# Query transposes moved into the score banks, two blocks at a time, and the second key head's stacks written in halves

## The chip, the cores and the metric

The kernel runs on one core of a Trainium2 chip. The metric is the device time of one execution in microseconds (us), lower is better; times below are medians of several executions. A core has a matrix engine (TensorE, PE in the rows, with its weight loads as PEld), a vector engine (VectorE, DVE), an activation engine (ScalarE, ACT), GpSimd (POOL) and a queue that issues transfers (SyncE, SP). PE writes its results into PSUM, eight banks of 512 float32 columns by 128 partitions; ACT and DVE read them from there. Each engine works through its own instructions in order.

## What is computed

Two layers of a decoder trunk over 1024 tokens with 16 meta tokens in front, 1040 rows of 1024 features, in float32. Cut to what matters:

```python
h = jnp.concatenate([jnp.broadcast_to(meta.astype(x.dtype)[None], (B, N_META, x.shape[-1])), x], axis=1)
for l in range(DEPTH):                      # DEPTH = 2
    h = hybrid_layer(h, cos, sin, ...)
return h[:, N_META:]

def hybrid_layer(x, ...):
    h = rms_norm(x, norm_g)
    z = h @ w_in                            # 1024 x 6408
    aq, ak, av, ag, mq, mk, mv, mi, mf, mo, mgate = jnp.split(z, split_points(), axis=-1)
    q = apply_partial_rope(rms_norm(aq, q_norm_g), cos, sin)    # 16 heads of 64
    k = apply_partial_rope(rms_norm(ak, k_norm_g), cos, sin)    # 2 key heads of 64
    ya = sliding_window_sink_attention(q, k, v, sink) * jax.nn.silu(ag)
    ...                                     # mLSTM on mq, mk, mv, gated: ym
    return x + jnp.concatenate([ya, ym], axis=-1) @ w_out

# sliding_window_sink_attention, for each block of 128 queries:
scores = einsum(qb, kb) * scale             # keys: 16 meta tokens, the block before, the block itself
scores = where(mask, scores, NEG)
m = maximum(scores.max(-1), sink_b)
e = exp(scores - m)
probs = e / (e.sum(-1) + exp(sink_b - m))
out = einsum(probs, vb)
```

## The kernel before

**Numbers as pairs.** Every float32 factor of a large product is split into a high part, rounded to the matrix engine's format fp32r, and a low part, the remainder. A product of two such pairs is three matmuls (high by high, high by low, low by high). ACT makes the high part by a copy, DVE or POOL the low part by a subtraction that reads the same source.

**Stages.** A layer runs: keys and values of all tokens (`kv_tasks`), then the attention of eight pairs of heads, then the mLSTM of four heads, then the output product. While the attention of one pair runs, PE also computes projections for later work: the gate of a pair of heads (`g_tasks`) beside even pairs, the queries of the next two pairs (`q_tasks`) beside odd ones, the mLSTM values beside pair 7. `weave` lays the two lists of tasks into each other, 24 or 25 foreground tasks (6 to 9 projection matmuls each) over one pair's steps, and PE's instructions stay in that order. The instructions of ACT, DVE and POOL are ordered by a scheduler when the program is built.

**One block of attention.** A pair has 9 blocks of 128 queries in layer 0 (block 0 is the 16 meta tokens), 8 in layer 1. For block b, `s1` writes the scores of both heads into one of two score tiles `S` (each two banks, one a head: four matmuls, L667), DVE puts the mask and the sink into them (L670, L681) and takes the maximum (L685), ACT makes the exponentials and their sum (L688), DVE the reciprocal (L690), ACT scales (L693). Two steps later `s2` transposes the probabilities into the one bank `T` (L704, L707), from which ACT (L711, L712) and DVE (L714, L715) make high and low parts. One step after that `s3` and `s4` multiply them with the values into the one bank `O` (L731, L743), from which ACT (L746) and DVE (L748) take the result. `s1` of block b + 2 writes the same score tile as block b. Of a score bank's 512 columns, 274 at most hold scores.

**PSUM.** Two banks are `S` tile 0, two `S` tile 1, one is `T`, one `O`, and two, named `pj`, take turns for everything else: the projections, and also the query transposes. A gate chunk is taken from its `pj` bank by a tanh on ACT and L640 on DVE.

**Queries.** `q_stacks(j, g)` makes the stationary operand of four blocks' scores for pair j: four transposes of 128 by 128 into one `pj` bank (L617), then `q_put`: two ACT copies of 64 partitions by 512 columns (L600, L601) and two DVE subtractions (L602, L603). It is called at foreground tasks 20 or 21 for the next pair's first half (g = 0, blocks 1 to 4) and 8 or 9 for the second (g = 1, blocks 5 to 8). The 16 meta queries go by a small transpose into columns of the `O` bank (L622) and the same four lines at 16 columns.

**Keys.** The key stacks `Ks` hold one of the two key heads at a time, both halves of the partitions. The second head's, for pairs 4 to 7, are written over the first's near the end of pair 3: `k_stacks(1, g, i)` is an ACT copy (L436) and a DVE subtraction (L437) of 64 partitions by 576 columns, four calls, after the scores of blocks (3, 6), (3, 7), (4, 1), (4, 2), with (pair, block) as in the source.

## Time and profile before

| what | us |
|---|---|
| median of 3 runs | 1950.03 (1949.86 to 1952.85) |
| the profiled execution | 1953.92 |
| its span, first to last instruction | 1952.2 |
| PE busy in it | 1908.1 (98%) |
| DVE, ACT, POOL busy | 1088.3, 1067.7, 906.4 |

The profiled execution is 3.89 us above the median of the three runs, and 1.72 us of it lie outside the span. Its granted TensorE clock is 0.998 over the span. In rows of the trace "idle before <- releaser" is the time for which an engine stood still before an instruction, and the engine and line that ended the wait. A PE row such as `x6` merges six matmuls of one form; a PE row's duration runs past the start of the next, since matmuls are pipelined.

### The profile page before, as it was taken

The page shows a single profiled execution, that of the slowest core. Times are in us where ns is not written, and L with a number is a line of the kernel's source. Part 1 is how long each engine was busy: PE and PEld are TensorE (multiplying, and loading weights), DVE is VectorE, ACT ScalarE, POOL GpSimd, SP SyncE. Part 2 cuts the span into 40 slices and gives each one's busy share as a digit, 9 for nine tenths or more (in the row PEclk, how much of TensorE's full clock was granted, in tenths as well). Part 3 has the DMA queues.
Part 4 walks back from the last instruction along what each step waited for, and adds up shares of the span by engine and source line. Part 5 has one row for each costly group of instructions (what it writes and reads, how often), then busy time and mean ns, then how long its engine had stood idle before and what let it go on. Part 6 is the DMA issues. An engine that isn't in the chain of part 4 may idle for free.

```text
span 1952.2 us, 36164 instructions
## 1 busy us (share of the span) xinstructions
PE 1908.1 (98%) x12827; PEld 1799.7 (92%) x12827; DVE 1088.3 (56%) x2966; ACT 1067.7 (55%) x3133; POOL 906.4 (46%) x1102
## 2 busy tenths in 40 slices
PE   8999999999999999999999999999999999999999
PEld 7998898999999999977789999999999999998887
DVE  7777777667454363532445678776673635437211
ACT  6577776747454544643334777776464535446221
POOL 3544544336545454564325345444365444547332
PEclk9999999999999999999999999999999999999999
DMA  4111111121222121455541111112122121226543
GB/s 153 44 37 49 39 43 35 37 65 35 62 60 58 41 56 55 146 164 168 176 132 50 39 37 54 43 36 59 39 58 64 40 67 50 57 62 187 171 149 121
DMA packets 150838, 148.28 MB, mean 76 GB/s; under 512 B 15081, under 2 KB 123921, under 8 KB 150658
## 3 DMA queue, kind: packets, MB, share of 16 engines
q1 hardware_dynamic: 150658, 145.97, 25.5%
q8 instruction: 101, 1.65, 0.4%
q14 instruction: 79, 0.65, 0.1%
HBM read 122.58 MB, written 23.29 MB: 75 GB/s over the span
## 4 chain that ended last, share of the span: by engine, by line
PE 80%; DVE 6%; ACT 4%; issue 3%; POOL 3%; DMA 3%; SPq 0%; POOLq 0%; DVEq 0%; ACTq 0%
PE pj L186 35%; PE pj L226 13%; PE pss L1204 6%; PE pj L1204 6%; PE po L1204 5%; PE po L917 2%; PE S L667 2%; PE pss L917 2%; DMA raw<-in_w_in_dram 2%; PE O L743 2%; POOL RING L160 1%; PE O L731 1%; PE pt L917 1%; ACT t L688 1%; PE T L707 1%
## 5 line engine op out<-in xcount | busy, mean ns | idle before, releaser
L186 PE MATMUL pj<-H,RING 128*128 128x384 f32 (+2 forms) x3456 | 583.0, 322 | 0.0
L186 PEld LDWEIGHTS pj<-H,RING 128*128 128x128 f32 x3456 | 543.3, 188 | 2.5 <-issue 0.2
L160 POOL TENSOR_TENSOR RING<-raw,RING 128x512 fp32r<-128x512 f32 (+1 forms) x192 | 255.5, 1338 | 121.5 <-ACT RING L159 114.4
L226 PE MATMUL pj<-RING,H 128*128 128x256 f32 (+1 forms) x1920 | 268.3, 286 | 3.5 <-DVE u L640 3.5
L226 PEld LDWEIGHTS pj<-RING,H 128*128 128x128 f32 x1920 | 242.5, 189 | 4.0 <-DVE u L640 3.8
L226 PE MATMUL pj<-H,RING 128*128 128x384 f32 (+2 forms) x1152 | 215.0, 326 | 3.9 <-DVE u L603 3.9
L186 PE MATMUL pj<-RING,H 128*128 128x256 f32 x1536 | 209.9, 287 | 3.3 <-DVE H L300 1.6
L178 POOL TENSOR_TENSOR RING<-raw,RING 128x512 fp32r<-128x512 f32 x96 | 125.9, 1318 | 175.8 <-ACT RING L177 167.3
L186 PEld LDWEIGHTS pj<-RING,H 128*128 128x128 f32 x1536 | 193.8, 191 | 6.1 <-DVE H L300 2.1
L226 PEld LDWEIGHTS pj<-H,RING 128*128 128x128 f32 x1152 | 179.4, 189 | 4.8 <-PE T L707 2.3
L177 ACT ACTIVATE RING<-raw 128x512 fp32r<-128x512 f32 x128 | 80.7, 631 | 173.0 <-DMA raw<-in_w_out_dram 139.6
L159 ACT ACTIVATE RING<-raw 128x512 fp32r<-128x512 f32 (+1 forms) x196 | 122.8, 630 | 66.1 <-DMA raw<-in_w_in_dram 50.4
L752 POOL TENSOR_TENSOR u<-u,w1k 128x128 f32<-128x128 f32 (+1 forms) x136 | 63.7, 468 | 172.7 <-DVE w1k L748 168.6
L688 ACT ACTIVATE t<-S,mx 128x145 f32<-128x145 f32 (+1 forms) x272 | 100.3, 373 | 59.8 <-DVE mx L685 52.7
L718 POOL TENSOR_SCALAR_AFFINE_SELECT p<-p 128x512 fp32r<-128x512 f32 x112 | 72.4, 646 | 126.9 <-DVE p L714 126.4
L930 POOL TENSOR_TENSOR p<-u,p 128x258 fp32r<-128x258 f32 x64 | 49.7, 777 | 170.8 <-ACT p L929 155.6
L1204 PE MATMUL pss<-RING,H 128*128 128x512 f32 x384 | 120.5, 394 | 0.0
L1204 PE MATMUL pj<-RING,H 128*128 128x512 f32 x352 | 110.7, 396 | 0.0
L693 ACT ACTIVATE t<-t,mx 128x144 f32<-128x144 f32 (+1 forms) x272 | 97.5, 407 | 20.3 <-DVE mx L690 20.1
L866 DVE SCALAR_TENSOR_TENSOR t<-u,cw,t 128x384 f32<-128x384 f32 (+1 forms) x144 | 107.2, 744 | 2.2
L886 DVE SCALAR_TENSOR_TENSOR t<-t,pj 128x384 f32<-128x384 f32 (+2 forms) x48 | 24.5, 511 | 124.8 <-ACT t L885 124.7
L748 DVE TENSOR_TENSOR w1k<-O,w1k 64x128 f32<-64x128 f32 (+1 forms) x272 | 74.6, 274 | 34.2 <-ACT w1k L746 31.3
(344 smaller groups left out, 3804.6 us busy)
## 6 DMA issues: line engine op xcount, KB each, us to landing
raw<-in_w_out_dram SPq DMA_DIRECT2D x128, 256.0 KB, 2.8
raw<-in_w_in_dram SPq DMA_DIRECT2D x100, 256.0 KB, 2.8
raw<-in_w_in_dram SPq DMA_DIRECT2D x192, 128.0 KB, 2.3
spool<-u SPq DMA_DIRECT2D x56, 192.0 KB, 1.9
p<-x SPq DMA_DIRECT2D x24, 256.0 KB, 3.6
t<-spool SPq DMA_DIRECT2D x30, 192.0 KB, 3.4
p<-spool SPq DMA_DIRECT2D x26, 192.0 KB, 4.2
u<-em SPq DMA_DIRECT2D x8, 576.0 KB, 6.5
```

The source lines that it names most:

```text
L159: sc.activation(hi, raw[:, :, 0:o], AF.Copy)
L160: eng.tensor_tensor(lo, raw[:, :, 0:o], hi, op=ALU.subtract)
L177: sc.activation(hi, raw, AF.Copy)
L178: (ve if i > 8 and i % 2 else gp).tensor_tensor(lo, raw, hi, op=ALU.subtract)
L186: last = pin(pe.matmul(out, a, b, start=(i == 0), stop=(i == n - 1)))
L226: pin(pe.matmul(out(), x, y, start=(k + i == 0), stop=(k == n - 1 and i == 2)))
L688: sc.activation(P[:p, 145 * h:145 * h + 145], S[:p, h, 1 + 127 * h:146 + 127 * h], AF.Exp, bias=mx[:p, 0, h:h + 1], accum_out=mx[:p, 1, h: ...
L693: sc.activation(Pn, Pn, AF.Copy, scale=mx[:p, 2, h:h + 1])
L748: ve.tensor_tensor(y[64 * h:64 * h + 64, :p], O[0:64, p * h:p * h + p], up[0:64, p * h:p * h + p], op=ALU.add)
L866: ve.scalar_tensor_tensor(z, RAW[:, t0 + i:t0 + i + n], wcol(i), z, ALU.mult, ALU.add)
L917: pin(f(*a, **k))
L1204: pin(pe.matmul(ps[:p, :], a, b, start=(i + n == 0), stop=(i == 15 and n == len(terms) - 1)))
```

## The change

Two things are moved. First, all of `q_stacks` but the very first of a layer becomes `q_turn` and `q_take`, called from `s1`: behind the score matmuls of a block named in `visits`, two transposes write the unused columns 384 to 512 of that block's two score banks, and once the block's softmax has been issued two ACT copies and two DVE subtractions of 64 partitions by 2 x 128 columns take them. A visit comes two blocks ahead of the first of the two blocks that it serves: blocks 8 of the pair before, 1, 3 and 5. There are 30 visits in each layer in place of 15 calls of `q_stacks`, with the same 60 transposes. Second, `k_stacks` takes a first block and a count, and the second key head is written in eight calls of 288 columns, after the scores of blocks (3, 6), (3, 7), (3, 8) and (4, 1) to (4, 5), by the table `KEYS`. As each is a task of the woven list, the foreground tasks of pairs 3 and 4 shift by one against the steps in places.

```diff
--- before.py
+++ after.py
@@ -34,6 +34,8 @@
 UW = 1152
 NPAIR = 8
 EARLY = 80
+KEYS = {(3, 6): (0, 2, 0), (3, 7): (0, 2, 1), (3, 8): (2, 2, 0), (4, 1): (2, 2, 1),
+        (4, 2): (4, 2, 0), (4, 3): (4, 2, 1), (4, 4): (6, 2, 0), (4, 5): (6, 2, 1)}
 FIRST = ((0, 0), (0, 1), (1, 0))
 
 
@@ -427,14 +429,14 @@
                 pin(pe.transpose(ps[:, 128 * i:128 * i + 128], KR[:, 4 * g + 1 + i, :], ident))
             sc.activation(KT[:, 4 * g:4 * g + 4, 16:144], ps[:, 0:512].rearrange("p (a c) -> p a c", a=4), AF.Copy)
 
-        def k_stacks(kv, g, i):
+        def k_stacks(kv, a, n, i):
 
             s0 = 64 * kv
-            src = KT[s0:s0 + 64, 4 * g:4 * g + 4].rearrange("p a c -> p (a c)")
+            src = KT[s0:s0 + 64, a:a + n].rearrange("p a c -> p (a c)")
             d = 64 - s0 if i else s0
-            hi, lo = [T[d:d + 64, 576 * g:576 * g + 576] for T in Ks]
+            hi, lo = [T[d:d + 64, 144 * a:144 * a + 144 * n] for T in Ks]
             sc.activation(hi, src, AF.Copy)
-            ve.tensor_tensor(lo, src, Ks[0][s0:s0 + 64, 576 * g:576 * g + 576], op=ALU.subtract)
+            ve.tensor_tensor(lo, src, Ks[0][s0:s0 + 64, 144 * a:144 * a + 144 * n], op=ALU.subtract)
 
         def v_stacks(kv, g):
 
@@ -617,6 +619,22 @@
                 pin(pe.transpose(ps[:, 128 * i:128 * i + 128], X[:, 256 * i + c0:256 * i + c0 + 128], ident))
             q_put(U[:, 0:1024], ps, 512)
 
+        def q_turn(S, j, g, i):
+
+            c0 = 128 * (j % 2)
+            X = A[j]["q"]["X", g == 1]
+            for k in range(2):
+                pin(pe.transpose(S[:, k, 384:512], X[:, 256 * (i + k) + c0:256 * (i + k) + c0 + 128], ident))
+
+        def q_take(S, j, g, i):
+
+            Q = q_unit(j, g)[:, 0:1024].rearrange("p (h a c) -> p h a c", h=2, a=4)[:, :, i:i + 2]
+            src = S[:, :, 384:512]
+            sc.activation(Q[0:64, 0], src[0:64], AF.Copy)
+            sc.activation(Q[64:128, 1], src[64:128], AF.Copy)
+            ve.tensor_tensor(Q[64:128, 0], src[0:64], Q[0:64, 0], op=ALU.subtract)
+            ve.tensor_tensor(Q[0:64, 1], src[64:128], Q[64:128, 1], op=ALU.subtract)
+
         def q_meta_turn(j, ps):
             c0 = 128 * (j % 2)
             pin(pe.transpose(ps, A[j]["q"]["XM"][:, c0:c0 + 128], ident[:16, :16]))
@@ -657,6 +675,7 @@
             def s1(b):
                 t0, p = TT[b]
                 S = SS[blk[0] % 2]
+                visit = visits.get(blk[0])
                 blk[0] += 1
                 k0, kn, o = (0, 16, 128) if b == 0 else (0, 144, 128) if b == 1 else (16 + (b - 2) * 144, 272, 0)
                 for h in range(2):
@@ -666,6 +685,8 @@
                     for i in range(2):
                         pin(pe.matmul(S[:p, h, o + 2 - 2 * h:o + 2 - 2 * h + kn], lq, Ks[i][:, k0:k0 + kn],
                                   start=(i == 0), stop=(i == 1)))
+                if visit:
+                    q_turn(S, *visit)
                 if st.setdefault("S", 0) < 2:
                     ve.tensor_copy(cols(S, 1, 783, 1), snk[:, l, 2 * j:2 * j + 2].rearrange("p (h c) -> p h c", c=1))
                 st["S"] += 1
@@ -691,6 +712,8 @@
                 for h in range(2):
                     Pn = P[:p, 1 + 144 * h:145 + 144 * h]
                     sc.activation(Pn, Pn, AF.Copy, scale=mx[:p, 2, h:h + 1])
+                if visit:
+                    q_take(S, *visit)
                 live[b] = P
 
             def s2(b):
@@ -1052,8 +1075,8 @@
         in_order[0] = True
         fq = q_tasks(0, wq[0], QQ[0])
         n0 = len(fq) - 24
-        at = {n0 + 6: [lambda: k_turn(0), lambda: (k_stacks(0, 0, 0), k_stacks(0, 0, 1)), lambda: v_stacks(0, 0)],
-              n0 + 15: [lambda: k_turn(1), lambda: (k_stacks(0, 1, 0), k_stacks(0, 1, 1)), lambda: v_stacks(0, 1)],
+        at = {n0 + 6: [lambda: k_turn(0), lambda: (k_stacks(0, 0, 4, 0), k_stacks(0, 0, 4, 1)), lambda: v_stacks(0, 0)],
+              n0 + 15: [lambda: k_turn(1), lambda: (k_stacks(0, 4, 4, 0), k_stacks(0, 4, 4, 1)), lambda: v_stacks(0, 1)],
               n0 + 21: [lambda: q_stacks(0, 0, "pss")] + ([lambda: q_meta(0, bank("po")[:, 0:16])] if first_q == 0 else [])}
         at[n0 + 12] = q_post(QQ[0], False)
         for i, f in enumerate(fq):
@@ -1065,6 +1088,8 @@
         SS[:] = [bp["S"].tile([128, 2, 512], F32, name=f"S{i}") for i in range(2)]
         steps = [(j, *x) for j in range(8) for x in att_tasks(j, A[j])]
         ns = len(steps) // 8
+        visits = {j * ns + 4 * g + i + 1 - first_q - 2: (j, g, i)
+                  for j in range(8) for g in range(2) for i in (0, 2) if j + g > 0}
 
         def step(i):
 
@@ -1072,8 +1097,9 @@
             if i < len(steps):
                 j, b, s1 = steps[i][:3]
                 out.append(lambda: s1(b))
-                if (j, b) in ((3, 6), (3, 7), (4, 1), (4, 2)):
-                    out.append(lambda: k_stacks(1, j - 3, b - 6 if j == 3 else b - 1))
+                k = KEYS.get((j, b))
+                if k:
+                    out.append(lambda: k_stacks(1, *k))
             if 0 <= i - 2 < len(steps):
                 b1, s2 = steps[i - 2][1], steps[i - 2][3]
                 out.append(lambda: s2(b1))
@@ -1103,11 +1129,6 @@
                 wg[0]()
             extra = len(fg) - 24 if j in (1, 3, 5) else 0
             at = {i: [nxt.more] for i in (3, 8, 12, 17)}
-            if j == 7:
-                at.setdefault(10, []).append(lambda: q_stacks(7, 1))
-            else:
-                at.setdefault((9 if j else 8) + extra, []).append(lambda j=j: q_stacks(j, 1))
-                at.setdefault(21 + extra if j % 2 else 20, []).append(lambda j=j: q_stacks(j + 1, 0))
             if j in (1, 3, 5):
                 for i, x in enumerate(q_post(QQ[j // 2 + 1], False)):
                     at.setdefault(13 + i + extra, []).append(x)
```

What the scheduler makes of it, in three places. Line numbers in rows of the changed kernel are its own: there L228 is the projection (L226 before), L686 the scores (L667), L727 and L730 the transposes to `T` (L704, L707), L766 and L754 the products into `O` (L743, L731), L702, L706 and L711 mask, maximum and reciprocal (L681, L685, L690), L737 and L738 the low parts from `T` (L714, L715), L771 the result (L748), L658 the gate (L640), L604 and L605 the meta queries' low parts (L602, L603), L439 the key stacks' low part (L437), L543 the scaling of queries (L541). L627 is the new transpose, L635 and L636 the new subtractions.

PE near the end of pair 0 in layer 0, before:

```order
L743 MATMUL O<-ptm_105,VM 128x128 x2
L743 MATMUL O<-p_1391,u 128x256 x2
L617 MATMUL pj<-cst,u 128x128 x4
L226 MATMUL pj<-H,RING 128x384 x6
L667 MATMUL S_1045<-u 128x272 x4
L704 MATMUL T<-cst,t 32x128
L707 MATMUL T<-cst,t 128x128 x2
```

and in the changed kernel:

```order
L766 MATMUL O<-ptm_105,VM 128x128 x2
L766 MATMUL O<-p_1394,u 128x256 x2
L228 MATMUL pj<-H,RING 128x384 x6
L686 MATMUL S_1045<-u 128x272 x4
L627 MATMUL S_1045<-cst,u 128x128 x2
L727 MATMUL T<-cst,t 32x128
L730 MATMUL T<-cst,t 128x128 x2
```

The four transposes left the `pj` bank and the place between two projections; two of them stand behind the scores, in their tile.

DVE over the same stretch, up to the gate of pair 0's last chunk, before:

```order
L681 COPY_PREDICATED S_1045<-mask,S_1045 128x2x128
L602 TENSOR_TENSOR u<-pj,u 64x512
L603 TENSOR_TENSOR u<-pj,u 64x512
L685 TENSOR_REDUCE mx<-S_1045 128x2
L714 TENSOR_TENSOR p_1513<-T,p_1513 128x256
L715 TENSOR_TENSOR ptm_105<-T,ptm_105 32x128
L748 TENSOR_TENSOR w1k<-O,w1k 64x128 x2
L690 RECIPROCAL mx<-mx 128x2
L640 SCALAR_TENSOR_TENSOR u<-t,pj 128x384
```

and after:

```order
L702 COPY_PREDICATED S_1045<-mask,S_1045 128x2x128
L706 TENSOR_REDUCE mx<-S_1045 128x2
L737 TENSOR_TENSOR p_1513<-T,p_1513 128x256
L738 TENSOR_TENSOR ptm_105<-T,ptm_105 32x128
L711 RECIPROCAL mx<-mx 128x2
L635 TENSOR_TENSOR u<-S_1045,u 64x256
L636 TENSOR_TENSOR u<-S_1045,u 64x256
L658 SCALAR_TENSOR_TENSOR u<-t,pj 128x384
L771 TENSOR_TENSOR w1k<-O,w1k 64x128 x2
```

The two 512-column subtractions are gone from the head of the row; two of 256 columns stand behind the reciprocal, and the result L748 (L771) stands behind the gate.

DVE in the middle of pair 1 in layer 0, where the meta queries are taken from the `O` bank and then the second half's queries are, before:

```order
L681 COPY_PREDICATED S_1045<-mask,S_1045 128x2x128
L685 TENSOR_REDUCE mx<-S_1045 128x2
L714 TENSOR_TENSOR p_2065<-T,p_2065 128x256
L715 TENSOR_TENSOR ptm_105<-T,ptm_105 32x128
L602 TENSOR_TENSOR u<-O,u 64x16
L603 TENSOR_TENSOR u<-O,u 64x16
L541 TENSOR_TENSOR u<-u,ssq__1996 128x512
L690 RECIPROCAL mx<-mx 128x2
L681 COPY_PREDICATED S_1046<-mask,S_1046 128x2x128
L602 TENSOR_TENSOR u<-pj,u 64x512
L603 TENSOR_TENSOR u<-pj,u 64x512
L685 TENSOR_REDUCE mx<-S_1046 128x2
L748 TENSOR_TENSOR w1k<-O,w1k 64x128 x2
```

and after:

```order
L702 COPY_PREDICATED S_1045<-mask,S_1045 128x2x128
L604 TENSOR_TENSOR u<-O,u 64x16
L605 TENSOR_TENSOR u<-O,u 64x16
L706 TENSOR_REDUCE mx<-S_1045 128x2
L737 TENSOR_TENSOR p_2074<-T,p_2074 128x256
L738 TENSOR_TENSOR ptm_105<-T,ptm_105 32x128
L543 TENSOR_TENSOR u<-u,ssq__2005 128x512
L711 RECIPROCAL mx<-mx 128x2
L702 COPY_PREDICATED S_1046<-mask,S_1046 128x2x128
L771 TENSOR_TENSOR w1k<-O,w1k 64x128 x2
L706 TENSOR_REDUCE mx<-S_1046 128x2
```

The meta queries' subtractions moved ahead of a maximum and of the two subtractions from `T`; behind the next mask no query subtraction stands any more ahead of the result from `O`.

DVE where pair 3 gives way to pair 4 in layer 0, before:

```order
L685 TENSOR_REDUCE mx<-S_1046 128x2
L602 TENSOR_TENSOR u<-pj,u 64x512
L603 TENSOR_TENSOR u<-pj,u 64x512
L437 TENSOR_TENSOR u<-u 64x576 x2
L690 RECIPROCAL mx<-mx 128x2
L670 COPY S_1045<-snk 128x2
L714 TENSOR_TENSOR p_3308<-T,p_3308 128x256
L715 TENSOR_TENSOR ptm_106<-T,ptm_106 32x128
```

and after:

```order
L771 TENSOR_TENSOR w1k<-O,w1k 64x128 x2
L702 COPY_PREDICATED S_1046<-mask,S_1046 128x2x128
L439 TENSOR_TENSOR u<-u 64x288 x2
L706 TENSOR_REDUCE mx<-S_1046 128x2
L711 RECIPROCAL mx<-mx 128x2
L737 TENSOR_TENSOR p_3328<-T,p_3328 128x256
L738 TENSOR_TENSOR ptm_106<-T,ptm_106 32x128
L635 TENSOR_TENSOR u<-S_1046,u 64x256
L636 TENSOR_TENSOR u<-S_1046,u 64x256
```

Of the 512-column and 576-column pairs that stood in a row, one 288-column pair and, three rows on, one 256-column pair are left.

## Rows read from the trace of the kernel before

**Rows 1.** The page, busy time, share of the span and number of instructions of the engines.

```profile
PE 1908.1 (98%) x12827; PEld 1799.7 (92%) x12827; DVE 1088.3 (56%) x2966; ACT 1067.7 (55%) x3133; POOL 906.4 (46%) x1102
```

**Rows 2.** Busy time of each engine in three stretches (their bounds, length, then busy us and instructions of PE, PEld, DVE, ACT, POOL, then granted clock, DMA share and GB/s): the attention of layer 0, that of layer 1, and a stretch of the mLSTM of layer 0.

```profile
78.00:405.00 327.00, 309.98 (x2363) 300.79 (x2362) 234.79 (x702) 234.77 (x793) 143.92 (x199) 0.99 0.15 42
1063.00:1362.00 299.00, 291.27 (x2260) 287.22 (x2259) 213.78 (x617) 216.14 (x705) 133.25 (x170) 1.00 0.16 44
500.00:800.00 300.00, 300.00 (x2070) 295.30 (x2069) 135.44 (x406) 146.76 (x425) 145.22 (x180) 1.00 0.21 55
```

**Rows 3.** Who PE waited for in the whole span: waiting line, releaser, us in total, times, longest.

```profile
PE O L731 <- DVE w1k L748: 6.4, 9, 1.7
PE T L704 <- DVE ptm L715: 5.5, 5, 1.7
PE pj L226 <- DVE u L603: 3.9, 5, 1.1
PE pj L226 <- DVE u L640: 3.5, 3, 1.3
PE O L731 <- DVE u L603: 2.8, 5, 1.1
...
PE pj L617 <- DVE u L640: 2.2, 2, 2.0
...
PE pj L210 <- DVE u L603: 0.5, 1, 0.5
```

**Rows 4.** PE in order of time at the start of layer 1's attention (start, us, engine, line, operation, out <- in, form, count, idle before and releaser).

```profile
1077.27 0.66 PE L617 MATMUL pj<-cst,u 128*128 128x128 f32 x4 [1.96 <-DVE u L640]
...
1082.24 0.27 PE L704 MATMUL T<-cst,t 128*32 128x128 f32 x1 [1.37 <-DVE ptm L715]
```

**Rows 5.** DVE in order of time at the same place.

```profile
1079.62 0.68 DVE L602 TENSOR_TENSOR u<-pj,u 64x512 fp32r<-64x512 f32 x1 [0.91 <-ACT u L601]
1080.32 0.69 DVE L603 TENSOR_TENSOR u<-pj,u 64x512 fp32r<-64x512 f32 x1
...
1081.38 0.42 DVE L714 TENSOR_TENSOR p<-T,p 128x256 fp32r<-128x256 f32 x1
1081.82 0.28 DVE L715 TENSOR_TENSOR ptm<-T,ptm 32x128 fp32r<-32x128 f32 x1
```

**Rows 6.** PE in layer 0 in order of time: the first projection after the last gate chunk of pair 0, and waits in the middle and at the end of odd pairs 1 and 5.

```profile
114.30 0.98 PE L226 MATMUL pj<-RING,H 128*128 128x256 f32 x6 [1.13 <-DVE u L640]
...
146.62 0.47 PE L731 MATMUL O<-p,u 128*128 128x256 f32 x2 [1.05 <-DVE u L603]
...
152.34 0.47 PE L731 MATMUL O<-p,u 128*128 128x256 f32 x2 [0.69 <-DVE w1k L748]
...
315.63 0.48 PE L731 MATMUL O<-p,u 128*128 128x256 f32 x2 [0.68 <-DVE w1k L748]
```

**Rows 7.** DVE in the middle of pair 1, in order of time.

```profile
145.00 0.46 DVE L685 TENSOR_REDUCE mx<-S 128x2 f32<-128x290 f32 x1
...
146.30 0.18 DVE L603 TENSOR_TENSOR u<-O,u 64x16 fp32r<-64x16 f32 x1
```

**Rows 8.** PE, then DVE, in order of time where pair 3 gives way to pair 4 in layer 0.

```profile
236.77 0.27 PE L704 MATMUL T<-cst,t 128*32 128x128 f32 x1 [0.88 <-DVE ptm L715]
...
238.95 0.57 PE L731 MATMUL O<-p,u 128*128 128x256 f32 x2 [1.69 <-DVE w1k L748]
...
233.31 1.96 DVE L437 TENSOR_TENSOR u<-u 64x576 fp32r<-64x576 f32 x2
```

**Rows 9.** The same place as busy time in stretches of 2 us (columns as in Rows 2).

```profile
236.00:238.00 2.00, 0.49 (x3) 0.28 (x3) 1.85 (x6) 1.98 (x6) 2.00 (x4) 1.00 0.25 45
238.00:240.00 2.00, 1.05 (x5) 1.08 (x6) 1.96 (x5) 1.98 (x9) 1.51 (x3) 0.79 0.31 106
240.00:242.00 2.00, 2.00 (x10) 2.00 (x10) 0.79 (x4) 1.80 (x5) 2.00 (x4) 0.50 0.39 93
```

**Rows 10.** Single lines over the whole span: line, engine, operation, count, then ns of one (least/median/most), first and last start, form; and in the last row what DVE stood idle for ahead of L602 (releaser, us in total, times).

```profile
L600 ACT ACTIVATE u<-pj x30: 570/592/594, 87.5 to 1337.2; 64x512 fp32r<-64x512 f32 x30
L600 ACT ACTIVATE u<-O x7: 161/177/178, 104.2 to 349.0; 64x16 fp32r<-64x16 f32 x7
...
L602 DVE TENSOR_TENSOR u<-pj,u x30: 677/684/685, 88.7 to 1338.4; 64x512 fp32r<-64x512 f32 x30
L602 DVE TENSOR_TENSOR u<-O,u x7: 167/168/169, 104.6 to 349.4; 64x16 fp32r<-64x16 f32 x7
...
L603 DVE TENSOR_TENSOR u<-pj,u x30: 693/693/694, 89.4 to 1339.1; 64x512 fp32r<-64x512 f32 x30
...
L437 DVE TENSOR_TENSOR u<-u x16: 743/752/1186, 59.4 to 1210.7; 64x576 fp32r<-64x576 f32 x16
...
  ACT u L601: 7.3, 17
```

**Rows 11.** PE in order of time: the four transposes and the next projection, at the end of pair 2.

```profile
188.65 0.60 PE L617 MATMUL pj<-cst,u 128*128 128x128 f32 x4
189.01 1.30 PE L226 MATMUL pj<-H,RING 128*128 128x384 f32 x6
```

**Rows 12.** The reciprocal of block 1 of pair 2 on DVE and the scores of block 3 on PE, in order of time.

```profile
164.99 0.17 DVE L690 RECIPROCAL mx<-mx 128x2 f32<-128x2 f32 x1 [0.41 <-ACT t L688]
...
166.83 0.67 PE L667 MATMUL S<-u 128*128 128x272 f32 x4
```

## The prediction

> **What bounds the kernel now.** I read the page first: PE is busy 1908.1 us of 1952.2, no other engine over 56% [rows 1]. Where PE waits for nothing it cannot be sped up by this change, which adds and drops no matmul; so only PE's idle time matters. The view by stretches says where that is: 327.0 - 309.98 = 17.0 us in the attention of layer 0, 299.0 - 291.27 = 7.7 us in that of layer 1, none in 300 us of the mLSTM, where DVE has far less to do (135 us against 215 to 235) [rows 2]. The view of who waited for whom names the releasers: nearly always a DVE line that empties a PSUM bank [rows 3]. So the question for each edit is whether it makes a bank free sooner at one of these some 25 waits, and which bank gets late instead.
>
> The profiled execution took 1953.92 us, the median is 1950.03. I make the sum as a difference on the profiled one and carry it to the median. [...]
>
> **Query transposes out of the pj banks: gain 4.4 + 2.2 + 1.0.** With a query bank between two projections, only one pj bank is left for them until DVE has done L602 and L603. PE waited for L603 before a projection 5 + 1 times, 3.9 + 0.5 = 4.4 us [rows 3]. The bank no longer passes through these lines: I count all 4.4. The transposes themselves waited for a bank held by a gate (L617 for L640) 2.2 us, of which 1.96 at the start of layer 1 [rows 3, 4]; the score tile that they now go to is already PE's own at that moment, so I count 2.2. Right behind, PE waited 1.37 us for the low part from `T`, and DVE shows why: L602 and L603, 0.68 + 0.69, stand just before [rows 4, 5]. They move behind the next reciprocal; PE also arrives earlier, so I count 1.0 and not 1.37.
>
> **What the scheduler makes of the freed DVE: gain 2.1 + 1.4 + 2.2.** The meta queries sit in the one `O` bank, and PE waited 2.8 us in five places for their low part L603; the long ones are 1.05 us [rows 3, 6]. In the changed order these subtractions stand ahead of a maximum and of the two subtractions from `T`, 0.46 + 0.42 + 0.28 = 1.16 us earlier [rows 5, 7]. I count two long waits, 2.1, and leave the short ones. The two waits of 0.69 and 0.68 us for the result from `O` (L748) come where two 512-column subtractions stood ahead of it in the queue; none does now: 1.4 [rows 6]. The three waits for the gate of a pair's last chunk, L640, sum to 3.5 [rows 3]. Ahead of it go 0.684 + 0.693 = 1.38 us of subtractions [rows 10] and come two at 256 columns. These I take on a straight line between 16 and 512 columns: 0.168 + (0.684 - 0.168) x 240 / 496 = 0.42 us, with L603 0.85 for the pair (0.69 if a half costs half, 1.38 if it costs the same as the whole). The result L748 moves behind the gate, but DVE has to sit out ACT's copies: L602 waited for the second ACT copy 7.3 us in 17 times, 0.43 each [rows 10]. So L640 comes some 0.7 us sooner: 3 x 0.7, with a little for the shorter ACT row, 2.2.
>
> **Keys in halves: gain 1.6.** Where pair 3 gives way to pair 4, PE stands for 0.88 + 1.69 = 2.57 us, and in front of it DVE worked through 0.68 + 0.69 of query and 1.96 us of key subtractions in a row, 3.3 us [rows 5, 8]. A single key subtraction is usually 0.752 [rows 10], so 1.5 of the 1.96 is work. Now one pair of 288 columns (2 x 0.45 on the same straight line) and one of 256 (0.85) are left there, 1.75, with a reciprocal between: 1.6 less, and I count that. The other half of the keys goes to steps in which DVE has no such row; DVE's idle time there covers it, and if it does not, its own 0.9 us are lost.
>
> [...]
>
> **What it adds: loss 4.9.** PE: the same 60 transposes a layer, in twos instead of fours. Four and the next projection start 0.36 us apart, 0.09 each, with no mark of a changeover [rows 11]: 0, at most 0.05 for each of the 30 more groups. DVE: 60 visits x 0.85 - 30 x 1.38 = 9.6 us more; ACT by the same line (0.177 + 0.415 x 240 / 496 = 0.38) 60 x 0.76 - 30 x 1.18 = 10.2 us more [rows 10]. DVE is busy 72% of the attention [rows 2], so most is hidden by its idle time; what shows is a bank that is emptied later because a visit stands in front. Before, 30 such rows of 1.38 us cost PE about 4.0 us outside the pj waits (0.69, 0.68, 1.37 and half of 2.57), 0.13 each. A visit is 0.61 of that length: 0.08 each, 60 x 0.08 = 4.9. Bounds: 0, and 0.13 x 60 = 7.8.
>
> SP and POOL: none of the moved steps issues a transfer, and POOL, 46% busy [rows 1], only gets its input from the same DVE lines, so I charge nothing there.
>
> **Sum.** 4.4 + 2.2 + 1.0 + 2.1 + 1.4 + 2.2 + 1.6 = 14.9, less 4.9: 10.0 us. On the profiled execution 1943.9, on the median 1940.0. With no loss and the clock kept, 14.9 + 1.4 = 16.3: 1933.7.
>
> **Rivals.**
> *The gain is passed on.* PE comes earlier and finds the next DVE line late, as DVE is the engine that sets the pace of layer 0's attention: then only what is read in layer 1's start (3.3) and little else stays, say 3 to 4 us with losses at their bound: 1946.5. For it: four different DVE lines share the releases [rows 3]. Against: DVE has 28% idle.
> *The bank is not what PE waited for.* The wait for L603 becomes a wait for L640 in the other pj bank, so the first 4.4 are lost: 10.0 - 4.4 = 5.6, 1944.4. For it: L640 already ends three such waits. Against: elsewhere the projections find their second bank free.
> *The queries come too late: slower.* The visit serves scores two blocks on, and the same score tile is written then. The thinnest place that I found: reciprocal of block 1 in pair 2 done at 165.16, scores of block 3 at 166.83, 1.67 us [rows 12]. In between must go the maximum of the next block (0.46) and the visit (0.85), 1.31, and the 0.43 for ACT if it is not hidden: 1.74. I take the other visits to have more. If all 60 came late by more than 14.9 / 60 = 0.25 us, the change loses; at 0.4 each it is 24.0 - 14.9 = 9.1 us, 1959.1.
> [...]
>
> **How the numbers follow.** A measurement of this kernel can tell about 0.2% from no change, 3.9 us: faster is under 1946.1, slower over 1953.9. Chances: forecast (around 1940, 1934 to 1946) 0.55; bank rival (1944.4) 0.15; gain passed on (1946.5, to 1951) 0.20; queries too late 0.10. Faster: 0.55 + 0.13 + 0.04 = 0.72; same: 0.02 + 0.16 = 0.18, with slower 0.10. The range goes from all gains without loss, 1933.5, to 1950.5 in the passed-on case; below and above lie about 0.07 and 0.12.
>
> **What would show it.** Right: no PE wait for the new subtractions before a projection, no wait of the transposes, PE's idle time in the two attention stretches down from 24.7 to about 15 us, no two waits at the change from pair 3 to 4. Passed on: the same sum of idle time under other names (L748, the low part from `T`). Queries too late: waits of PE's scores for the new subtractions or copies. The forecast is wrong if the scheduler's new order makes waits where there were none, above all in odd pairs of layer 0.

## The result and the profile after

The changed kernel took 1957.84 us (median of 10 runs, 1954.44 to 1965.23), the kernel before 1952.65 beside it: a ratio of 1.0036, 95% interval 1.0026 to 1.0046. Ratios, here and below, leave out slow runs (one of the kernel before took 2533.33 us) and are not the quotients of the medians, which is 1.0027 here. It is **slower by 5 us (medians) to 7 us (ratio)**, where 10 us less were predicted. The profiled execution took 1959.92 us, with a span of 1958.2 (before 1952.2).

Line numbers move with the change: the matmul with the values into `O` is L754 (before L731), the O result that empties the bank L769 on ACT and L771 on DVE (L746, L748), the meta queries' copies L602 to L605 (L600 to L603), scaling L543 and turning L553, L557, L558 (L541, L551, L555, L556), the visits' copies L633 to L636, the key halves L438 and L439, GpSimd's low part of the weights L162. Experiment kernels shift a few lines more; the operation and the tiles in a row tell which it is.

The page's busy line, to be read against [rows 1]:

```profile
PE 1909.9 (98%) x12827; PEld 1802.7 (92%) x12827; DVE 1099.7 (56%) x3034; ACT 1074.6 (55%) x3201; POOL 910.6 (47%) x1102
```

PE's idle time is 1958.2 - 1909.9 = 48.3 us, where it was 44.1, and its busy time is 1.8 us longer for the same matmuls: of the 6.0 us by which the profiled span grew, 4.2 are idle and 1.8 are matmuls at a lower granted clock (0.995 for 0.998 over the span). The two attention stretches, as [rows 2]:

```profile
78.00:405.00 327.00, 308.51 (x2347) 299.90 (x2346) 236.47 (x731) 238.27 (x826) 143.84 (x196) 0.99 0.15 41
1063.00:1362.00 299.00, 289.17 (x2217) 285.57 (x2217) 220.43 (x644) 213.09 (x725) 130.26 (x165) 0.98 0.15 42
```

Both have more idle PE than before, 18.5 + 9.8 = 28.3 us for 24.7, and the clock of layer 1's stretch fell from 1.00 to 0.98. Who PE waited for, as [rows 3]:

```profile
PE O L754 <- DVE S L691: 8.8, 4, 3.6
PE O L754 <- DVE w1k L771: 6.8, 9, 1.3
PE O L754 <- ACT t L714: 3.1, 1, 3.1
PE T L727 <- DVE ptm L738: 2.8, 3, 1.6
...
PE O L754 <- DVE u L848: 2.1, 1, 2.1
PE O L754 <- ACT ptm L735: 1.8, 2, 1.2
...
PE O L754 <- DVE u L605: 1.1, 1, 1.1
PE O L640 <- DVE w1k L771: 1.1, 2, 0.5
...
PE pj L228 <- DVE u L658: 0.4, 1, 0.4
```

The waits for `pj` are gone but for 0.4 us, as predicted. In their place stand waits for the one `O` bank, under many releasers' names (a wait is put down to the last event; `S L691` is the instruction behind the O result). I sum PE's idle time by the bank that it waited to write, over both attention stretches, from PE's rows in order of time, for the kernels that the argument needs (us):

| kernel | pj | T | O | S |
|---|---|---|---|---|
| before | 10.1 | 3.7 | 10.1 | 0.6 |
| after | 0.4 | 1.2 | 24.9 | 1.5 |
| copies halved, old place | 27.9 | 1.7 | 4.6 | 0.8 |
| all work held behind O | 0 | 1.8 | 17.4 | 20.6 |
| scaling behind O | 0.6 | 0.2 | 17.5 | 5.5 |
| meta queries moved | 3.4 | 1.2 | 18.2 | 2.9 |
| order and meta | 0.8 | 3.7 | 9.9 | 6.4 |

By layers, `O` rose from 8.2 to 15.5 us in layer 0 and from 1.9 to 9.4 in layer 1, about half of the 14.8 us in each.

**The two kinds of long wait.** At the start of layer 1's pair 2, PE stands for 3.32 us. DVE, PE, ACT and POOL there, in order of time:

```profile
1138.55 0.56 DVE L771 TENSOR_TENSOR w1k<-O,w1k 64x128 f32<-64x128 f32 x2
...
1140.07 1.76 DVE L543 TENSOR_TENSOR u<-u,ssq__14119 128x512 f32<-128x512 f32 x1
...
1142.60 1.59 DVE L553 TENSOR_TENSOR t<-u,qrt 128x128 f32<-128x128 f32 x2
1144.22 0.42 DVE L635 TENSOR_TENSOR u<-S,u 64x256 fp32r<-64x256 f32 x1
1144.65 0.43 DVE L636 TENSOR_TENSOR u<-S,u 64x256 fp32r<-64x256 f32 x1
1145.11 0.42 DVE L658 SCALAR_TENSOR_TENSOR u<-t,pj 128x256 f32<-128x256 f32 x1
1145.44 0.42 DVE L557 TENSOR_TENSOR u<-u,qrt 128x256 f32<-128x256 f32 x1
1145.78 0.57 DVE L771 TENSOR_TENSOR w1k<-O,w1k 64x128 f32<-64x128 f32 x2
```

```profile
1139.80 0.46 PE L766 MATMUL O<-p,u 128*128 128x256 f32 x2
...
1146.50 0.77 PE L754 MATMUL O<-p,u 128*128 128x256 f32 x2 [3.32 <-DVE S L691]
```

```profile
1142.35 0.38 ACT L769 ACTIVATE w1k<-O 64x256 f32<-64x256 f32 x1
```

```profile
1140.00 1.28 POOL L162 TENSOR_TENSOR RING<-raw,RING 128x512 fp32r<-128x512 f32 x1
...
1142.12 1.28 POOL L162 TENSOR_TENSOR RING<-raw,RING 128x512 fp32r<-128x512 f32 x1
```

The product was done at 1140.26, its result comes off DVE at 1146.35, though ACT's half had been copied by 1142.73. Ahead of it on DVE stand the second half's scaling and turning, and a visit's two subtractions. Two of these, 1.76 and 1.59 us, are long just where POOL subtracts beside them; the scaling took 0.69 us at 220.18, with no GpSimd row beside it. Of this kind are also 1.07 us at 1224.17 and 3.57 us at 1297.73 (pairs 4 and 6). In layer 0 a visit and other lines stand ahead of the 1.33 us at 155.21 and the 1.34 us at 320.75; scaling and turning come behind. The other kind falls at block 3 of a head pair in layer 0, where the next pair's meta queries sit in `O`. DVE, then PE, then ACT, in pair 3:

```profile
226.00 0.57 DVE L771 TENSOR_TENSOR w1k<-O,w1k 64x128 f32<-64x128 f32 x2
226.60 0.17 DVE L579 TENSOR_SCALAR ssq__3203<-ssq__3203 128x8 f32<-128x8 f32 x1
226.87 1.02 DVE L439 TENSOR_TENSOR u<-u 64x288 fp32r<-64x288 f32 x2
227.93 0.42 DVE L737 TENSOR_TENSOR p<-T,p 128x256 fp32r<-128x256 f32 x1
228.39 0.28 DVE L738 TENSOR_TENSOR ptm<-T,ptm 32x128 fp32r<-32x128 f32 x1
228.74 0.17 DVE L711 RECIPROCAL mx<-mx 128x2 f32<-128x2 f32 x1
228.99 0.17 DVE L604 TENSOR_TENSOR u<-O,u 64x16 fp32r<-64x16 f32 x1
229.17 0.17 DVE L605 TENSOR_TENSOR u<-O,u 64x16 fp32r<-64x16 f32 x1
```

```profile
229.49 0.47 PE L754 MATMUL O<-p,u 128*128 128x256 f32 x2 [3.06 <-ACT t L714]
```

```profile
226.40 0.91 ACT L438 ACTIVATE u<-u 64x288 fp32r<-64x288 f32 x2
...
228.60 0.17 ACT L602 ACTIVATE u<-O 64x16 fp32r<-64x16 f32 x1
228.78 0.18 ACT L603 ACTIVATE u<-O 64x16 fp32r<-64x16 f32 x1
```

The O result was out at 226.57; the bank comes free only with L605, 2.8 us later. On DVE a key half and four more lines stand between, but DVE was not the only one late: ACT, with its own key half and other work ahead, made the meta queries' copies that L604 and L605 read only at 228.60 to 228.96.

### The profile page after: what moved, and what is told of

Its sections match the earlier page's. It is cut to its first block, busy times and chain, and to the rows that moved or that the text cites. A ratio compares the mean times of both kernels' runs of the same rounds, so it can differ in the third digit from the quotient of the medians.

```text
span 1958.2 us, 36279 instructions
## 1 busy us (share of the span) xinstructions
PE 1909.9 (98%) x12827; PEld 1802.7 (92%) x12827; DVE 1099.7 (56%) x3034; ACT 1074.6 (55%) x3201; POOL 910.6 (47%) x1102
## 4 chain that ended last, share of the span: by engine, by line
PE 78%; DVE 6%; ACT 5%; issue 4%; POOL 3%; DMA 3%; SPq 0%; POOLq 0%; ACTq 0%; DVEq 0%
PE pj L188 34%; PE pj L228 14%; PE pss L1225 6%; PE pj L1225 5%; PE po L1225 5%; PE S L686 2%; PE po L940 2%; PE pss L940 2%; PE O L766 2%; DMA raw<-in_w_in_dram 2%; POOL RING L162 1%; PE O L754 1%; PE pt L940 1%; PE T L730 1%; ACT t L709 1%
## 5 line engine op out<-in xcount | busy, mean ns | idle before, releaser
L162 POOL TENSOR_TENSOR RING<-raw,RING 128x512 fp32r<-128x512 f32 (+1 forms) x192 | 255.8, 1339 | 115.8 <-ACT RING L161 111.8
L228 PE MATMUL pj<-RING,H 128*128 128x256 f32 (+1 forms) x1920 | 269.1, 286 | 0.4 <-DVE u L658 0.4
L228 PEld LDWEIGHTS pj<-RING,H 128*128 128x128 f32 x1920 | 242.9, 189 | 0.8 <-DVE u L658 0.5
L228 PE MATMUL pj<-H,RING 128*128 128x384 f32 (+2 forms) x1152 | 218.4, 329 | 0.0
L228 PEld LDWEIGHTS pj<-H,RING 128*128 128x128 f32 x1152 | 181.9, 192 | 0.0
L714 ACT ACTIVATE t<-t,mx 128x144 f32<-128x144 f32 (+1 forms) x272 | 98.1, 408 | 10.3 <-DVE mx L711 9.5
L771 DVE TENSOR_TENSOR w1k<-O,w1k 64x128 f32<-64x128 f32 (+1 forms) x272 | 74.6, 274 | 30.1 <-ACT w1k L769 27.3
```

The costliest lines, as they stand in the source:

```text
L162: eng.tensor_tensor(lo, raw[:, :, 0:o], hi, op=ALU.subtract)
L228: pin(pe.matmul(out(), x, y, start=(k + i == 0), stop=(k == n - 1 and i == 2)))
L714: sc.activation(Pn, Pn, AF.Copy, scale=mx[:p, 2, h:h + 1])
L771: ve.tensor_tensor(y[64 * h:64 * h + 64, :p], O[0:64, p * h:p * h + p], up[0:64, p * h:p * h + p], op=ALU.add)
```

## The experiments

Theories: **order** (the scheduler now puts other work ahead of what empties `O`), **amount** (60 visits' worth of extra instructions), **GpSimd** (VectorE's instructions are long while GpSimd works, and that is what makes the order dear), and **any rearrangement costs** in a tuned order. Each ratio is to the kernel before on the same chip, so the difference of two kernels' ratios has an uncertainty of 0.0013 to 0.0018, by their intervals.

**Halves of the change.** The keys whole again in the changed kernel, and the key halves alone in the kernel before:

```
-KEYS = {(3, 6): (0, 2, 0), (3, 7): (0, 2, 1), (3, 8): (2, 2, 0), (4, 1): (2, 2, 1), ...}
+KEYS = {(3, 6): (0, 4, 0), (3, 7): (0, 4, 1), (4, 1): (4, 4, 0), (4, 2): (4, 4, 1)}
```

> The changed kernel with the second key head's stacks written as before, in four whole parts (at blocks 6 and 7 of head pair 3 and 1 and 2 of head pair 4); only the query visits remain of the change. The whole change measured 1.0036 of the kernel before (+7 us). If the visits bring the loss, this stays at +4 to +8 us (1.002 to 1.004), with the long waits for the O bank at the start of layer 1's head pairs (3.3 and 3.6 us in the changed kernel) still there. If the key halves bring it, the 3 us wait near 229 us goes and the time falls to -1 to -6 us (0.997 to 0.9995).

> The kernel before with the key halves alone; the queries are transposed in fours into the pj bank as before. If the visits bring the loss, this is the kernel before less at most 1.6 us for the halved copies: 1951 to 1953.5 (0.9990 to 1.0005). If the key halves bring it, +3 to +8 us (1.0015 to 1.004), with a wait of about 3 us on TensorE near 229 us.

Visits only: 1.0036 (1.0022 to 1.0049); the waits at 1146 and 1298 us are there. Keys only: 1.0017 (1.0008 to 1.0025), with a wait of 3.30 us near 231 us. The visits bring the loss, but I had given the key halves alone none: they are dear where they stand ahead of the meta queries. On top of the visits they change nothing that can be told (1.0036 both): with whole keys PE waits 0.89 us near 227 and 2.75 near 238 us, with halves 3.06 and 1.32.

**The amount of work at the old place.**

```
-            q_put(U[:, 0:1024], ps, 512)
+            for c in (0, 256):  # the same four copies, columns c to c + 256 of each head
+                ...
```

> The kernel before with each copy of a four-block query stack written in two halves, at its old place and from the pj bank: the same number and size of ScalarE and VectorE instructions as the visits have, without the visits. If the amount of work (60 more pairs of visits' instructions, some 10 us on each of the two engines) brings the loss, +4 to +8 us (1.002 to 1.004). If the order does, within 2 us of the kernel before (0.999 to 1.001), and the waits for the O bank stay near the 10 us of the kernel before.

1.0090 (1.0075 to 1.0105), in the direction of "amount" and far past it. Yet the table shows where: pj from 10.1 to 27.9 us, `O` down to 4.6. At the old place, more instructions lengthened the wait for the bank that they empty, and made no waits for `O`. So the number of instructions alone doesn't explain the new O waits; but the order theory's "within 2 us" missed how dear a longer hold of a pj bank is.

**Everything held back behind the O result.**

```
-                    q_take(S, *visit)
+                    held_back.append(lambda: q_take(S, *visit))
...
+                with tc.issue_after(mark["O"]):   # at the end of the step's O result
+                    while held_back: held_back.pop(0)()
-                at.setdefault(1 + i, []).append(x)      # scaling and turning
+                at.setdefault(1 + i, []).append((lambda x=x: held_back.append(x)) if j else x)
```

> The changed kernel, all its work kept, with one thing moved: the scaling and turning of the next queries and the visits' copies are held until the result of the product with the values has been taken from the O bank in the same step, and on VectorE they are queued behind that result. If the loss is the order on VectorE (the O bank's release queued behind that work), the O-bank waits fall from 25 us to under 14 and the time by 6 to 12 us against the changed kernel: 0.997 to 1.0005 of the kernel before. If it is the amount of work, the time stays at 1.003 to 1.0045.

1.0137 (1.0121 to 1.0154), against the order theory as I had put it. The row that says why:

```profile
PE S L628 <- DVE u L559: 17.2, 6, 4.6
```

Held back by a step, the turned queries come too late for the visit that transposes them. That is a relative of the forecast's rival "queries too late" (there the scores wait for the visit's copies, here the visit's transposes wait for the turning), made by my edit, and it shows that this work has a due time on both sides.

**The late half's scaling and turning.** First spread by two token tiles, then left out, in both kernels:

> The changed kernel with the scaling and turning of the second half of the next queries done by two token tiles: that of tiles 5 and 6 in the odd head pair, as soon as they are projected, and only that of tiles 7 and 8 at the start of the even pair, where the visits to blocks 3 and 5 stand. The same elements in 4 more instructions per pair of heads. If the O bank's release is held up by the scaling and turning that meets the visits at the start of the even pairs (waits at 155, 241, 320, 1146, 1224 and 1298 us, 12 us together), those waits fall to under 5 us and the time by 6 to 11 us against the changed kernel: 0.998 to 1.0005 of the kernel before. If the visits' own copies hold it up, the waits stay and the time is at 1.003 to 1.005.

> The changed kernel without the scaling and turning of the second half of the queries for head pairs 2 to 7 (both layers; this part of the computation is left out, 4 VectorE steps per two pairs). If that work at the start of the even pairs is what the O bank's release queues behind, the waits for O at 155, 241, 320, 1146, 1224 and 1298 us go and the time is 10 to 16 us under the changed kernel: 0.995 to 0.9985 of the kernel before. If the visits' copies alone do it, at most 3 us go: 1.002 to 1.004.

> The kernel before without the scaling and turning of the second half of the queries for head pairs 2 to 7 (this part of the computation is left out). The changed kernel without it measured 0.9957, some 15 us under the changed kernel. If that work costs the changed kernel its time because it meets the visits, leaving it out gives the kernel before far less: 0 to 6 us, 0.997 to 1.0. If it costs both kernels alike, 0.991 to 0.995.

Spread: 1.0099 (1.0085 to 1.0113), outside both of my ranges. The collision only moved; DVE and PE there:

```profile
1149.07 1.54 DVE L543 TENSOR_TENSOR u<-u,ssq__14139 128x512 f32<-128x512 f32 x1
...
1150.65 1.76 DVE L553 TENSOR_TENSOR t<-u,qrt 128x64 f32<-128x64 f32 x2
```

```profile
1154.59 0.77 PE L763 MATMUL O<-p,u 128*128 128x256 f32 x2 [3.69 <-DVE S L700]
```

Half the elements took as long (1.76 us for two of 64 columns, 1.59 for two of 128 in the changed kernel), so cutting the work didn't shorten it. Left out: 0.9957 (0.9945 to 0.9970) in the changed kernel, 0.9962 (0.9949 to 0.9974) in the one before. With this work the change costs 0.36%, without it -0.05%, which is none that can be told: **the loss needs the visits and the scaling together** (0.41% between the two differences, with an uncertainty of 0.2). The kernel before gained more by it, 0.38% or 7 us, than the 0 to 6 us that I had allowed. The O waits are not all gone with it: 15.6 us are left in the changed kernel and 7.0 in the one before, against pj waits of 1.3 and 7.6.

**A rearrangement as such, and GpSimd by a later load.**

```
-            at = {i: [nxt.more] for i in (3, 8, 12, 17)}
+            at = {i: [nxt.more] for i in (6, 9, 13, 18)}
```

> The changed kernel with the four weight loads of each head pair issued at the 7th, 10th, 14th and 19th part of the projection instead of the 4th, 9th, 13th and 18th, so that GpSimd's subtraction of the first pair of weights comes after the scaling and turning at the start of the even pairs. If VectorE's instructions there are long (1.6 to 1.9 us in place of 0.5 to 0.7) because GpSimd works beside them and the O bank waits for that, the waits at 1146 and 1298 us fall from 3.4 to under 1.5 us each and the time by 4 to 9 us: 0.999 to 1.0015. If only the order of VectorE's queue counts, they stay over 2 us and the time is at 1.002 to 1.005.

> The kernel before with the same shift of the weight loads, and nothing of the change. If the kernel before is an order in which any rearrangement costs some microseconds, this is 2 to 8 us slower: 1.001 to 1.004. If the loss of the changed kernel comes from the visits meeting the scaling and turning, this is within 2 us: 0.999 to 1.001.

In the changed kernel 1.0044 (1.0029 to 1.0058), in the kernel before 0.9997 (0.9987 to 1.0007). This rearrangement cost the kernel before nothing; that any would do is not borne out (key halves did cost it 0.17%, by a wait that can be named). On GpSimd it is inconclusive: its two subtractions still lay beside the scaling, which took 1.77 us, and the wait stayed 3.32.

**A finer order.** Scaling and turning stay where they are written, save the second step, which is written two parts later, and queue behind the latest O result; the visits' copies and key halves go behind the O result of their own step. All, the first part, the second part:

```
+        def after_o(f):
+            with tc.issue_after(mark["O"]) if "O" in mark else nullcontext():
+                f()
-                at.setdefault(1 + i, []).append(x)
+                at.setdefault((1, 3, 3, 4)[i], []).append(lambda x=x: after_o(x))
...
-                out += [lambda: s3(b2), lambda: s4(b2)]
+                out += [lambda: s3(b2), lambda: (s4(b2), flush())]   # copies and keys, behind O
```

> The changed kernel, all its work kept, in a finer order than the attempt before: the scaling and turning stays where it is written (its second step two parts later), and is queued on VectorE behind the latest O result that is written ahead of it; the visits' copies and the key halves are written behind the O result of the same step, on ScalarE behind its copy and on VectorE behind its sum. In the changed kernel the turned queries were ready 5 us before the visit that reads them, so this should not bring the transposes' wait back. If the loss is the order (the O bank's release behind this work), the waits at 155, 229, 241, 320, 1146 and 1298 us, 14 us together, fall to under 6 us and the time by 8 to 15 us against the changed kernel: 0.996 to 1.0. If it is the amount of work, 1.002 to 1.005.

> Of the kernel with the finer order only the scaling and turning moved, the visits' copies and the key halves as in the changed kernel. If the scaling and turning is the work that stands ahead of the O result, the waits at 1146 and 1298 us fall from 3.4 us each to under 1.5 and the time to 0.999 to 1.002 of the kernel before; the wait at 229 us (key halves) stays. If the visits' copies matter as much, the fall is under 2 us: 1.002 to 1.004.

> The other part of the finer order: only the visits' copies and the key halves are written behind the O result of their step, the scaling and turning as in the changed kernel. If the scaling and turning is what holds the O bank, the waits at 1146 and 1298 us stay over 2 us, the one at 229 us (3.1 us, key halves) falls to under 1.5, and the time is 1.001 to 1.004. If the visits' copies are, those waits fall too and the time is 0.997 to 1.0005.

All: 1.0027 (1.0018 to 1.0036); scaling and turning alone: 1.0008 (0.9999 to 1.0018); copies and keys alone: 1.0029 (1.0016 to 1.0041). With the same work and only its place in the queue changed, the middle one gives back 0.28% of the 0.36. Its waits at 1146 and 1298 us for `O` are gone, since the O result now leads, and shorter ones for the turned queries are left. DVE at pair 2, then PE at pair 6, of layer 1:

```profile
1145.05 0.58 DVE L772 TENSOR_TENSOR w1k<-O,w1k 64x128 f32<-64x128 f32 x2
1145.66 0.84 DVE L544 TENSOR_TENSOR u<-u,ssq__14119 128x512 f32<-128x512 f32 x1
```

```profile
1298.64 0.44 PE L628 MATMUL S<-cst,u 128*128 128x128 f32 x2 [1.57 <-DVE u L559]
```

The O waits fall in layer 1, from 9.4 to 2.1 us, with 4.8 us of waits for `S` in exchange; layer 0 keeps 15.4. The third brought 0.07%, less than can be told. Its O waits at 1146 and 1298 us halved all the same, to 1.67 and 1.74 us, so the visits' copies were part of what stood ahead; waits for the score banks came up in their place (7.5 us). The time is that of my first case for it, the waits are not. Both parts together did worse than the scaling alone, against the order theory's number for them. In both kernels that hold the copies, two of the meta queries' waits grew (in the first 2.06 us for 1.09 near 106, 2.31 for 1.17 near 188), and a wait of 2.2 us for a visit's copies came up near 1086, in layer 1's first steps, where no O result is written and the copies were held for a step.

**The meta queries out of `O`.** Into a free column of block 6's score bank: on top of the scaling's order, in the changed kernel alone, in the kernel before.

```
-                if b == 3 and j < 7 and first_q == 0:
-                    st["QM"] = O[:, 256:272]
-                    q_meta_turn(j + 1, st["QM"])
+                QM = S[:, 0, 384:400] if b == 6 and j < 7 and first_q == 0 else None
+                if QM is not None: q_meta_turn(j + 1, QM)    # copied behind this block's softmax
```

> The kernel with the scaling and turning behind the O result (measured 1.0008), and the next pair's meta queries transposed into a free column of the score bank of block 6 in place of the O bank of block 3, and copied from there. If the meta queries' copies are what holds the O bank at block 3 (waits at 106, 187, 231 and 355 us, 8.8 us together, and smaller ones in every pair of layer 0), those waits fall to under 3 us and the time by 5 to 10 us: 0.9955 to 0.9985 of the kernel before. If the O result itself is late there (key halves and weight copies ahead of it on ScalarE), they stay and the time is at 1.000 to 1.002.

> The changed kernel with the meta queries in the score bank of block 6, and the scaling and turning as in the changed kernel. If the meta queries hold the O bank at block 3, the waits at 106, 186, 229 and 353 us fall, the ones of layer 1 at 1146 and 1298 us stay, and the time falls by 4 to 9 us from 1.0036: 0.999 to 1.0016. If not, 1.003 to 1.0045.

> The kernel before with the meta queries in the score bank of block 6 alone. Its waits for O behind the meta queries' copies were 2.8 us in 5. If they are a cost by themselves, 2 to 5 us go: 0.9975 to 0.999. If it is only in the changed kernel that they meet other copies, 0.999 to 1.001.

0.9990 (0.9977 to 1.0003), 1.0024 (1.0011 to 1.0036), 0.9991 (0.9981 to 1.0001). The waits at 106, 186 and 353 us go, and the one at 229 shrinks; the key half (L439, from 227.00) now comes behind the O result (226.39 to 226.96), which alone empties the bank:

```profile
227.11 0.47 PE L756 MATMUL O<-p,u 128*128 128x256 f32 x2 [0.72 <-DVE w1k L773]
```

So in these places the bank was held by the meta queries, as the rows had it. The worth is small: 0.18% on top of the scaling's order, just clear of the noise, and 0.12 and 0.09% in the other two, which are not. It is less than I expected: as the O waits fall by 6.7 us in the changed kernel, those for pj come back from 0.4 to 3.4 (table).

**Both orders and the meta queries,** with the copies not held in a layer's first three steps; and the changed kernel without GpSimd's subtraction:

> The kernel with the scaling and turning behind the O result and the meta queries in the score bank of block 6 (measured 0.999), with the visits' copies and the key halves also written behind the O result of their step, save in the first three steps of a layer, where no O result is written. If ScalarE's and VectorE's copies of the visits ahead of the O result's copy are the rest (waits at 155, 225, 236 and 317 us, 6.3 us together), the time falls by 3 to 7 us, to 0.9955 to 0.998. If the visits' copies come too late for the scores then, waits for those take their place and the time is at 0.999 to 1.002.

> The changed kernel without GpSimd's subtraction that makes the low halves of the weights loaded in head pairs 1 to 7 (this part of the computation is left out; the products are still formed, from the halves that stand in the ring). VectorE's order at the start of layer 1's pairs 2 and 6 is the same as in the changed kernel. If GpSimd beside it is what makes VectorE's scaling and turning 1.6 to 1.8 us long, these take 0.5 to 0.9 us, the waits at 1146 and 1298 us fall from 3.4 to under 1.7 us each, and the time by 3 to 9 us: 0.999 to 1.002. If the order alone makes the waits, the instructions stay long or the waits stay over 2.8 us, and the time is within 3 us of the changed kernel: 1.002 to 1.005.

Order and meta: 1948.56 us against 1953.61, **0.9977 (0.9967 to 0.9987): faster than both kernels**, the clock 1.00 in both stretches:

```profile
78.00:405.00 327.00, 314.06 (x2395) 304.84 (x2394) 240.19 (x746) 241.84 (x830) 149.63 (x202) 1.00 0.16 43
1063.00:1362.00 299.00, 290.66 (x2258) 286.43 (x2257) 217.62 (x655) 221.99 (x742) 138.14 (x172) 1.00 0.17 46
```

Without GpSimd's subtraction: 0.9997 (0.9988 to 1.0007), 0.39% under the changed kernel. The run has its own control, by luck: at the start of pair 6 GpSimd still makes the wider low parts for the next stage, and I had expected both waits to fall. DVE at pair 2 and at pair 6, where the scaling, the turning and a visit stand ahead of the O result in both (the lines between differ a little), then PE:

```profile
1143.16 0.91 DVE L545 TENSOR_TENSOR u<-u,ssq__14091 128x512 f32<-128x512 f32 x1
1144.11 0.49 DVE L555 TENSOR_TENSOR t<-u,qrt 128x128 f32<-128x128 f32 x2
...
1287.76 1.80 DVE L545 TENSOR_TENSOR u<-u,ssq__16271 128x512 f32<-128x512 f32 x1
1290.24 1.72 DVE L555 TENSOR_TENSOR t<-u,qrt 128x128 f32<-128x128 f32 x2
```

```profile
1146.91 0.47 PE L756 MATMUL O<-p,u 128*128 128x256 f32 x2 [1.02 <-DVE S L693]
...
1294.47 0.48 PE L756 MATMUL O<-p,u 128*128 128x256 f32 x2 [3.20 <-DVE S L693]
```

The wait falls from 3.32 to 1.02 us where GpSimd's subtraction is left out and stays at 3.20 where it is not; the two rows are 1.95 us shorter together (1.76 + 1.59 against 0.91 + 0.49). So order alone is worth about 1 us there, and GpSimd beside VectorE the other 2.3: the long wait at pair 2 needs both, and the 1.07 us at pair 4 is gone too. In layer 0 the O waits hardly change, 14.3 us for 15.5. Queueing this work behind the O result and leaving GpSimd's out each came out most of the loss lower, but the kernel before was run with neither, so how much it would have gained too, and so how much of the 0.28 and 0.39% belongs to the change, is not shown. By its O waits in layer 1 it had little to give, 1.9 us against 9.4.

## Why the prediction was wrong

- **Query transposes out of the pj banks** (gains of 4.4 and 2.2) and the gates' waits (2.2): right. The pj waits fell by 9.7 us, 8.8 were counted. The wait behind them for `T` was counted at 1.0; `T` fell by 2.5.
- **"What the scheduler makes of the freed DVE", gains of 2.1 and 1.4 at the O bank:** right where I had looked, wrong for the bank. The four waits that I counted (1.05 and 0.69 us in pair 1, 1.05 and 0.68 in pair 5) are gone, but I took these places for all: the O waits as a whole rose by 14.8 us.
- **"What it adds: loss 4.9": the step that failed.** It priced a visit by a mean, 0.08 us, on the argument that DVE is idle 28% of the stretch. The waits weren't spread like that: two places in layer 1, where the late scaling, a visit and GpSimd meet ahead of the O result, cost 3.32 and 3.57 us, one in layer 0, where a key half stands ahead of the meta queries, 3.06, and 0.13 x 60 = 7.8 was no upper bound. With this loss and the gains of 2.1 and 1.4, `O` was to come out at most 4.9 - 3.5 = 1.4 us worse; it came out 14.8 worse, more than the 12.2 us that pj and `T` gave back.
- **Keys in halves, 1.6:** the two waits at the change of pairs did shrink to 1.32 us, but 3.06 came up at 229 us, and the run with whole keys shows no net gain. "DVE's idle time covers it" looked at DVE's load and not at what waits behind it, there and on ACT: the meta queries in the only O bank.
- **"SP and POOL: I charge nothing":** wrong for POOL. Scaling and turning now meet GpSimd's subtractions ahead of an O result, for some 2.3 us at pair 2 of layer 1. The kernel before had one such place already, and I had not seen it: L541 took 1.86 us at 157.71, ahead of the O result at 160.69 for which PE then waited 1.07 us.
- **The clock kept, 1.4 us at the end of the range:** no run shows this term; it was my estimate, 2 x 0.21 + 2 x 0.50 by the clocks of 0.79 and 0.50 in [rows 9]. Between 236 and 244 us, with one wait of 1.32 us, the changed kernel's clock stayed at 1.00, but over the span it went the other way, 0.995 for 0.998, and cost 1.8 us in the profiled execution.
- **Rivals.** "The gain is passed on" named the mechanism, the next bank found late, but stopped it at a small gain; nothing in its reasoning limits it there. "The bank is not what PE waited for" fell (pj 0.4). "Queries too late" was not what made this kernel slower: the waits for `S` rose by 0.9 us. A relative of it decided the run with all work held back. The mask waited for the transposes into its score banks: of DVE's 26 waits for PE before a mask in the two stretches of the changed kernel, 17 end with the transposes, 10.3 us together. The forecast's last sentence, new waits by the scheduler's order, is what happened, at the start of even pairs more than in odd ones.

Of the predicted gain of 10 us, 0.23% or some 4.5 us are had once the O waits are back where they were (9.9 us, before 10.1). How much of that is the change's own isn't shown: the meta queries' move alone took 0.09% off the kernel before, within the noise, and the order was not tried there. Where the rest went isn't settled either: that version still has 6.4 us of waits for the score banks, most of them for the turned queries of layer 1, and moving those visits wasn't tried.

## What to carry to other kernels

When work is moved off one bank, list every bank with a single buffer, and read from the new order what now stands ahead of the instruction that empties it; a mean price per instruction does not show such places. Small tenants of such a bank (here 16 columns of meta queries) held it as late as their last copy, at 229 us 2.8 us past the O result, so look for another place for them; here that was worth 0.2% at most. Before a VectorE row like the scaling, with both operands in SBUF, is counted as short, look whether GpSimd works beside it: here it took 0.69 us alone and up to 1.81 beside it.
